# When the next block of dense weights is fetched ahead of the prompt's latent attention: a two-layer hybrid encoder on one core

## The chip, the core and the metric

The kernel is one program on one core of a Trainium2 chip. A core has TensorE (PE in the profile, with its weight loads as PEld), VectorE (DVE), ScalarE (ACT), GpSimd (POOL) and SyncE (SP). Each engine takes its own instructions in order and waits for the others by semaphores; transfers are issued by SP and by POOL. The metric is the device time of one execution in microseconds (us), as the median of several runs.

## The reference, cut to what matters

Two layers run over a prompt of 1024 tokens and over 8 samples of 16 tokens, 1152 tokens in all. All numbers are f32.

```python
xn   = rms_norm(x, g)                                  # 1024 features
proj = xn @ w_in[l]                                    # 7072 columns, split into
c_q, c_kv, k_r, z_mla, q_d, k_d, v_d, z_diff, x_lru, z_lru, gate_logits = pieces
# latent attention: 8 heads, chunk-causal, softmax over the visible keys
s     = q_lat . c_kv + q_rope . k_rope
o_mla = softmax(s * 96**-0.5) . c_kv -> w_uv, times silu(z_mla)
o_diff = ...                                           # differential attention, times silu(z_diff)
o_lru  = ...                                           # gated recurrence, times silu(z_lru)
g      = sigmoid(gate_logits)                          # 3 branches x 1024
x      = x + (sum_b g_b * (o_b @ w_o_b)) @ w_out
```

## The kernel before, in words

Every product that needs f32 accuracy is made of three matmuls: each operand is split into a high part and the rest (`hi`, `lo`), and hi·hi, lo·hi and hi·lo are added up in PSUM (lines 200 to 202 of the profile).

The projections that nobody needs at once (the four 128-column blocks of z for each branch and the eight 128-column blocks of gate logits for each branch) are *dense tasks*. They stand in one list, in a fixed order, and fill TensorE's time beside work that waits for other engines. A dense task has two parts. Its *load* (`wload`, line 230) fetches a weight block of 512 KB from `w_in` by one transfer on SP's queue into a staging tile `gs`, which has one buffer; ScalarE casts it to the high part `gh` (line 237, 128x1024); GpSimd subtracts in four pieces to get the low part `gl` (line 240). `gh` and `gl` have two buffers each. Its *run* goes over the 1152 tokens in three chunks of 384: 24 matmuls, then ScalarE's tanh from PSUM into a tile `th` (line 662 for a gate, line 637 for z), and a store of `th` by SP (line 663 for a gate, line 646 for z). `th` has four buffers, so the tanh of a chunk waits for the store of the fourth chunk before it to land.

`_advance` (line 86) does one step of the first task in the list. If the task has not begun it makes its load and begins it. Then it makes the load of the *second* task in the list, if that has not been made:

```python
        if len(self.tasks) > 1:
            self._load(self.tasks[1])
```

So one block is always fetched ahead. Who calls `_advance` is decided by credit: `weave` (line 149) interleaves generators and gives `fill` (line 115) some us of credit for each of their steps; `fill` advances dense tasks until the credit is used up.

An attention goes through `pipeline` (line 880). Work is cut into units (head h, query group g of 256 tokens); the scores of a unit run `lag` units ahead of its values. For the prompt's latent attention (`mla`, line 938) lag is 2 and `wide` is set. The order there is:

1. the loads of head 0 are issued on GpSimd's queue (`head`, line 953: parts of kT and qT, then V), and `fill(burst)` gives 13.5 us of credit at once: the *dense burst* (line 905);
2. the scores of units (0,0) and (0,1) are written, beside dense work;
3. `pause` (line 913) advances the running dense task to the end of its chunk, and from then on `wide` is 1: no dense work is given out, and the scores use five PSUM banks (three `sc`, two of the dense work's, named `scm`);
4. for the last two units `wide` is 0 again and dense work resumes (line 935).

In the burst of each layer the last z block of the latent attention's branch ends and gate block 0 of that branch, here G0, begins. G1, G2 and G3 are the gate blocks that follow. G0's own load is made well ahead, when the last z block begins.

The softmax of a score tile (`soft`, line 796) is a maximum on VectorE (line 811 with the mask, line 813 without) and an exponential on ScalarE (line 821, `P`). The tiles are then transposed on TensorE (`pt`, lines 838 to 845), split on ScalarE and VectorE (`ph`, `pl`), and multiplied with V (`po`, lines 860 to 864).

The code yields instructions with priorities, and a scheduler sets each engine's order from these by a plan of its own. A load that is written late can so stand early on its engine where it depends on nothing that comes late: G2's and G3's loads are written after the attention, but stand on SP before its first output.

Of the kernel before, what the change touches and what calls it, by code (L numbers as in the profile page):

```python
# [42 lines left out]
class Net:  # L43
# [23 lines left out]
    def __init__(self, ctx, tc, i, o, depth=DEPTH, only=None):  # L67
        self.ctx, self.tc, self.i, self.o = ctx, tc, i, o
        self.nc = tc.nc
        self.depth = depth  # L70
        self.only = only
        self.tasks, self.done, self.credit = [], set(), 0.0
        self.weight = [0.0] * 6
        self.turn = 0
        self.wide = 0
        self.under_way = False


    def add_task(self, key, load, run):
# [6 lines left out]
    def _advance(self):  # L86
        t = self.tasks[0]
        if t[4] is None:
            self._load(t)
            t[4] = t[2](*t[3])  # L90
        if len(self.tasks) > 1:
            self._load(self.tasks[1])
        try:
            return self.behind(self.LATER[0], t[4])
        except StopIteration:
            self.tasks.pop(0)
            self.done.add(t[0])
            return 0.0
# [781 lines left out]
    def pipeline(self, units, heads, prep, scores, values, us, burst=0.0, lag=1, steps=None, wide=False):  # L880

        keys = []
        for u in units:
            k, _ = heads(u)
            if k is not None and k not in keys:
                keys.append(k)
        gens = {}

        def start(j):
            if j < len(keys) and keys[j] not in gens:
                u = next(u for u in units if heads(u)[0] == keys[j])
                gens[keys[j]] = heads(u)[1]()

        def finish(k):
            if k in gens:
                self.weave([gens[k]], us)

        n = len(units)  # L900
        edge = self.EDGE
        start(0)
        if keys:
            next(gens[keys[0]])
            self.fill(burst)
            self.weave([gens[keys[0]]], edge)
        self.weave([prep(units[0])], edge)
        for k in range(lag):
            self.weave([scores(units[k])], edge)
            finish(heads(units[k + 1])[0])  # L910
            self.weave([prep(units[k + 1])], us)
        if wide:
            self.pause()
            self.wide = 1
        for k, u in enumerate(units):
            own, rates, later = [values(u)], [1.0], [self.LATER[2]]
            if k + lag < n:
                own = [scores(units[k + lag])] + own
                later = [self.LATER[1]] + later
                if steps:  # L920
                    rates = [1.0, steps(u)[1] / steps(units[k + lag])[0]]
                else:
                    rates = [1.0, 1.0]
            if k + lag + 1 < n:
                finish(heads(units[k + lag + 1])[0])
                own.append(prep(units[k + lag + 1]))
                rates.append(1.0)
                later.append(self.LATER[3])
            ahead = None
            if heads(u)[0] is not None:  # L930
                j = keys.index(heads(u)[0]) + 1
                start(j)
                ahead = gens[keys[j]] if j < len(keys) else None
            if k + lag >= n:
                self.wide = 0
            self.weave(own, 0.0 if self.wide else us if k + lag < n else edge, ahead, rates, later)
# [787 lines left out]
```

## Time and profile before

| what | value |
|---|---|
| median of 3 runs | 3026.06 us (3023.16 to 3031.2) |
| the profiled execution's own time | 3023.51 us |
| its span, first to last instruction | 3021.6 us |
| TensorE busy | 2857.7 us, 95% |
| VectorE busy | 1651.7 us, 55% |
| ScalarE busy | 1395.0 us, 46% |
| GpSimd busy | 772.8 us, 26% |
| transfers | 396.89 MB, mean 131 GB/s |

TensorE's share is near full in most of the 40 slices of the page, so a change elsewhere counts where TensorE stands still. The latent attention of the prompt begins at about 957 us in layer 0 and at about 2459 us in layer 1; "idle before" in a row is the time in which that engine stood still before the instruction, and the name behind the arrow is what it waited for. The granted clock of TensorE is shown as a share of full speed.

### The profile page before, as it was taken

To read this page: it belongs to the slowest core of one execution; us is meant where nothing else is said; L and a number is where in the kernel's file an instruction comes from. 1 tells how busy PE (TensorE), PEld (TensorE's weight loads), DVE (VectorE), ACT (ScalarE), POOL (GpSimd) and SP (SyncE) were. 2 spreads that over 40 slices of the span, in tenths; PEclk is the share of its full clock that TensorE was granted. 3 is DMA by queue.
4 is the path that set the end of the run, shared out by engine and by line. 5 is a ranking of instruction groups with operands and counts; after the bars stand their busy time and mean duration, and the time that the engine had idled before them with its cause. 6 is when DMAs were issued, how large, how long until landed. Compare 5 with 4: busy or idle time off the path is not lost. (4 is left out here: it accounts for less than half of the span.)

```text
span 3021.6 us, 50750 instructions
## 1 busy us (share of the span) xinstructions
PE 2857.7 (95%) x18466; PEld 2705.9 (90%) x18466; DVE 1651.7 (55%) x3947; ACT 1395.0 (46%) x3367; POOL 772.8 (26%) x1132
## 2 busy tenths in 40 slices
PE   7999999999998999999989999999999989999998
PEld 7899899999897888999989998999999978889998
DVE  6322878747255855555343328777561557545543
ACT  4433766646333765312234347666452447542121
POOL 2221335120102113352131313342101111133620
PEclk9999999999999999999999999999999999999999
DMA  5434545265248533764133345452642584427541
GB/s 168 129 98 106 125 111 140 69 180 164 75 124 246 123 81 84 220 184 162 63 116 125 92 116 126 113 142 64 190 141 79 161 215 119 95 76 231 171 156 73
DMA packets 387658, 396.89 MB, mean 131 GB/s; under 512 B 56192, under 2 KB 342496, under 8 KB 386344
## 3 DMA queue, kind: packets, MB, share of 16 engines
q1 hardware_dynamic: 368048, 331.70, 36.7%
q0 software_dynamic: 19360, 61.95, 9.2%
q8 instruction: 146, 2.39, 0.3%
q14 instruction: 104, 0.85, 0.1%
HBM read 265.89 MB, written 127.66 MB: 130 GB/s over the span
## 5 line engine op out<-in xcount | busy, mean ns | idle before, releaser
L200 PE MATMUL pg<-xh,gh 128*128 128x384 f32 x1152 | 401.2, 348 | 7.5 <-ACT th L662 7.5
L821 ACT ACTIVATE P<-sc,mx 128x384 f32<-128x384 f32 (+4 forms) x598 | 335.5, 566 | 130.7 <-DVE mx L811 100.2
L201 PE MATMUL pg<-xl,gh 128*128 128x384 f32 x1152 | 395.8, 344 | 0.0
L202 PE MATMUL pg<-xh,gl 128*128 128x384 f32 x1152 | 395.3, 343 | 0.0
L240 POOL TENSOR_TENSOR gl<-gs,gh 128x256 fp32r<-128x256 f32 x288 | 230.3, 829 | 585.8 <-ACT gh L237 527.3
L194 DVE TENSOR_TENSOR pl<-pt,ph 128x512 fp32r<-128x512 f32 (+1 forms) x320 | 199.6, 634 | 53.2 <-ACT ph L193 50.8
L200 PEld LDWEIGHTS pg<-xh,gh 128*128 128x128 f32 x1152 | 218.2, 189 | 11.4 <-ACT th L662 9.2
L201 PEld LDWEIGHTS pg<-xl,gh 128*128 128x128 f32 x1152 | 218.1, 189 | 2.7
L202 PEld LDWEIGHTS pg<-xh,gl 128*128 128x128 f32 x1152 | 218.1, 189 | 0.9
L193 ACT CAST ph<-pt 128x512 fp32r<-128x512 f32 (+1 forms) x320 | 169.5, 544 | 81.8 <-PE pt L845 80.1
L200 PE MATMUL z<-xh,gh 128*128 128x384 f32 x576 | 203.3, 353 | 0.0
L201 PE MATMUL z<-xl,gh 128*128 128x384 f32 x576 | 199.6, 346 | 0.0
L202 PE MATMUL z<-xh,gl 128*128 128x384 f32 x576 | 198.4, 344 | 0.0
L200 PE MATMUL sc<-wyh,xh 128*128 128x256 f32 x576 | 163.0, 283 | 5.8 <-DVE xt L1550 5.8
L200 PE MATMUL dp<-wh,xh 128*128 128x256 f32 x576 | 165.2, 287 | 3.4 <-ACT e L575 2.1
L201 PE MATMUL dp<-wl,xh 128*128 128x256 f32 x576 | 164.4, 285 | 0.8 <-POOL wl L555 0.8
L202 PE MATMUL dp<-wh,xl 128*128 128x256 f32 x576 | 164.3, 285 | 0.0
L202 PE MATMUL sc<-wyh,ml 128*128 128x256 f32 x576 | 162.9, 283 | 0.0
L201 PE MATMUL sc<-wyl,xh 128*128 128x256 f32 x576 | 162.9, 283 | 0.0
L1235 PE MATMUL sc<-kT,qT 98*128 98x384 f32 (+3 forms) x384 | 140.6, 375 | 5.2 <-ACT P L821 4.6
L240 POOL TENSOR_TENSOR wol<-wos,woh 128x128 fp32r<-128x128 f32 x192 | 101.0, 554 | 172.2 <-ACT woh L237 153.6
L813 DVE TENSOR_REDUCE mx<-sc 128x1 f32<-128x384 f32 (+2 forms) x200 | 116.0, 586 | 39.1 <-PE sc L202 21.0
(456 smaller groups left out, 8355.3 us busy)
## 6 DMA issues: line engine op xcount, KB each, us to landing
gs<-in_w_in_dram SPq DMA_DIRECT2D x72, 512.0 KB
ts<-th SPq DMA_DIRECT2D x144, 192.0 KB
th<-ts SPq DMA_DIRECT2D x144, 192.0 KB
K<-in_cache_diff_k_dram SPq DMA_DIRECT2D x64, 256.0 KB
Vt<-in_cache_diff_v_dram SPq DMA_DIRECT2D x32, 512.0 KB
u<-ob SPq DMA_DIRECT2D x48, 288.0 KB
ws<-in_w_in_dram SPq DMA_DIRECT2D x24, 512.0 KB
z<-th SPq DMA_DIRECT2D x48, 192.0 KB
```

The source lines that it names most:

```text
L193: nc.scalar.copy(hi, src)
L194: (lo_engine or nc.vector).tensor_tensor(lo, src, rr(hi), op=ALU.subtract)
L200: nc.tensor.matmul(out, ah, bh, start=start and k == 0, stop=False)
L201: nc.tensor.matmul(out, ah, bl, start=False, stop=False)
L202: nc.tensor.matmul(out, al, bh, start=False, stop=stop and k == n - 1)
L240: (lo_engine or nc.gpsimd).tensor_tensor(lo[:, k : k + half], st[:, k : k + half], rr(hi[:, k : k + half]), op=ALU.subtract)
L813: nc.vector.tensor_reduce(mx, sc[:, : n1 - n0], axis=AX.X, op=ALU.max, negate=True)
L821: nc.scalar.activation(P[:, n0:n1], scs[k][:, : n1 - n0], AF.Exp, bias=mx, scale=1.0 if adds[k] is None else -1.0, accum_out=l2[:, k : k + 1])
L1235: nc.tensor.matmul(ps, lhs, kT[:, m, n0:n1], start=True, stop=True)
```

## The change

A flag `hold` is set when the dense burst of a `wide` pipeline begins and is taken back after `pause`. While it is set, `_advance` does not make the load of the second task. The flag is false for the two other users of `pipeline`.

```diff
         self.under_way = False
+        self.hold = False
...
-        if len(self.tasks) > 1:
+        if len(self.tasks) > 1 and not self.hold:
             self._load(self.tasks[1])
...
             next(gens[keys[0]])
+            self.hold = wide
             self.fill(burst)
...
             self.pause()
+            self.hold = False
             self.wide = 1
```

One load per layer is made at another point of the program: G1's, which was made in the burst when G0 began, is now made when dense work resumes at the end of the attention. No instruction is added or taken away. The scheduler places the moved instructions by its plan, and this is where they stand in layer 0; layer 1 has the same rows with other numbers. Line numbers of the kernel with the change are one higher up to its line 905, and two or three higher behind it.

SP's queue, from the last stores of z (`z0_0_111`) to the weight blocks fetched ahead. Before, `gs_10568` is G1, `gs_12497` G2 and `gs_12822` G3; `ts0_0_121` are the stores of G0's three chunks:

```order
L646 DMA z0_0_111<-th_10403 128x384
L236 DMA gs_10568<-in_w_in_dram 128x8x128
L646 DMA z0_0_111<-th_10506 128x384
L646 DMA z0_0_111<-th_10535 128x384
L663 DMA ts0_0_121<-th_10609 128x384
L646 DMA z0_0_111<-th_10564 128x384
L663 DMA ts0_0_121<-th_10661 128x384
L663 DMA ts0_0_121<-th_10690 128x384
L236 DMA gs_12497<-in_w_in_dram 128x8x128
L236 DMA gs_12822<-in_w_in_dram 128x8x128
```

The same queue with the change, where `gs_12488` is G1:

```order
L647 DMA z0_0_111<-th_10403 128x384
L647 DMA z0_0_111<-th_10506 128x384
L647 DMA z0_0_111<-th_10535 128x384
L647 DMA z0_0_111<-th_10564 128x384
L237 DMA gs_12488<-in_w_in_dram 128x8x128
L664 DMA ts0_0_121<-th_10600 128x384
L664 DMA ts0_0_121<-th_10652 128x384
L664 DMA ts0_0_121<-th_10681 128x384
L237 DMA gs_12497<-in_w_in_dram 128x8x128
L237 DMA gs_12822<-in_w_in_dram 128x8x128
```

G1's fetch has moved behind three stores of z, and all four stores of z now stand ahead of G0's; the fetches of G2 and G3 keep their places.

ScalarE at the start of the attention before: G0's three tanh (`th<-pg`), the cast of G1 (`gh_10569`), the first exponentials (`P`), and among them the cast of G2 (`gh_12498`):

```order
L662 ACTIVATE th_10609<-pg_10577 128x384
L237 CAST gh_10569<-gs_10568 128x1024
L662 ACTIVATE th_10661<-pg_10612 128x384
L662 ACTIVATE th_10690<-pg_10664 128x384
L821 ACTIVATE P_10602,lsum_10474<-sc_10603,mx_10607 128x128
L821 ACTIVATE P_10620,lsum_10474<-sc_10621,mx_10625 128x256
L821 ACTIVATE P_10637,lsum_10474<-sc_10638,mx_10642 128x384
L237 CAST gh_12498<-gs_12497 128x1024
L821 ACTIVATE P_10654,lsum_10474<-sc_10655,mx_10659 128x512
L821 ACTIVATE P_10698,lsum_10474<-scm_10699,mx_10718 128x384
```

The same place with the change; G1's cast is `gh_12489`:

```order
L663 ACTIVATE th_10600<-pg_10568 128x384
L663 ACTIVATE th_10652<-pg_10603 128x384
L238 CAST gh_12489<-gs_12488 128x1024
L663 ACTIVATE th_10681<-pg_10655 128x384
L822 ACTIVATE P_10593,lsum_10474<-sc_10594,mx_10598 128x128
L822 ACTIVATE P_10611,lsum_10474<-sc_10612,mx_10616 128x256
L822 ACTIVATE P_10628,lsum_10474<-sc_10629,mx_10633 128x384
L822 ACTIVATE P_10645,lsum_10474<-sc_10646,mx_10650 128x512
L822 ACTIVATE P_10689,lsum_10474<-scm_10690,mx_10709 128x384
```

G1's cast stands one tanh later, and no cast stands among the first exponentials. G2's cast is now some 30 rows further on, within head 1:

```order
L822 ACTIVATE P_10953,lsum_10474<-sc_10954,mx_10964 128x384
L822 ACTIVATE P_10953,lsum_10474<-scm_10960,mx_10964 128x384
L877 COPY hv_10921<-po_10860 64x256
L238 CAST gh_12498<-gs_12497 128x1024
L822 ACTIVATE P_10975,lsum_10474<-sc_10976,mx_11004 128x512
```

Nothing else stands there on ScalarE but the attention's own exponentials and splits.

GpSimd before, from head 0's V on: four pieces of G1's low part (`gl_10570`), the loads of head 1 (`kT1`, `qT1`, `V`), those of head 2 (`kT0`, `qT0`), and G2's low part (`gl_12499`):

```order
L960 DMA V_10486<-vm0_95 128x1024
L240 TENSOR_TENSOR gl_10570<-gs_10568,gh_10569 128x256 x4
L957 DMA kT1_10477<-kn0_91 64x2048
L958 DMA qT1_10479<-qn0_87 64x2x1024
L959 DMA qT1_10479<-qr0_89 32x2x1024
L960 DMA V_10693<-vm0_95 128x1024
L957 DMA kT0_10476<-kn0_91 64x2048
L958 DMA qT0_10478<-qn0_87 64x2x1024
L959 DMA qT0_10478<-qr0_89 32x2x1024
L240 TENSOR_TENSOR gl_12499<-gs_12497,gh_12498 128x256 x4
L960 DMA V_10933<-vm0_95 128x1024
```

The same queue with the change, up to head 3's first load:

```order
L963 DMA V_10486<-vm0_95 128x1024
L960 DMA kT1_10477<-kn0_91 64x2048
L961 DMA qT1_10479<-qn0_87 64x2x1024
L962 DMA qT1_10479<-qr0_89 32x2x1024
L963 DMA V_10684<-vm0_95 128x1024
L960 DMA kT0_10476<-kn0_91 64x2048
L961 DMA qT0_10478<-qn0_87 64x2x1024
L962 DMA qT0_10478<-qr0_89 32x2x1024
L241 TENSOR_TENSOR gl_12490<-gs_12488,gh_12489 128x256 x4
L963 DMA V_10924<-vm0_95 128x1024
L241 TENSOR_TENSOR gl_12499<-gs_12497,gh_12498 128x256 x3
L960 DMA kT1_10477<-kn0_91 64x2048
```

Head 1's loads now follow head 0's V at once, G1's low part stands behind head 2's loads of k and q, and three pieces of G2's low part stand ahead of head 3's loads.

## Rows read from the trace of the kernel before

**Rows 1.** Who waited for whom, the whole run: total us, times, longest us.

```profile
ACT gh L237 <- DMA gs<-in_w_in_dram: 52.9, 14, 9.7
```

**Rows 2.** Timeline of ScalarE, 957 to 973 us: start us, us, engine, line, operation [idle before].

```profile
957.29 0.49 ACT L662 ACTIVATE th<-pg 128x384 f32<-128x384 f32 x1 [3.53 <-PE pg L202]
...
969.07 1.04 ACT L237 CAST gh<-gs 128x1024 fp32r<-128x1024 f32 x1 [9.24 <-DMA gs<-in_w_in_dram]
970.02 0.68 ACT L821 ACTIVATE P<-sc,mx 128x512 f32<-128x512 f32 x1
...
972.25 0.59 ACT L821 ACTIVATE P<-scm,mx 128x384 f32<-128x384 f32 x1
```

**Rows 3.** Timeline of TensorE, 961 to 971 us.

```profile
970.85 0.80 PE L200 MATMUL sc<-kT,qT 128*128 128x512 f32 x1 [9.20 <-ACT P L821]
```

**Rows 4.** Timeline of VectorE, 957 to 973 us.

```profile
959.63 0.70 DVE L811 CUSTOM_DVE_ANT_0 sc<-sc,mask 128x512 f32<-128x512 f32 x1 [0.51 <-PE sc L202]
...
962.63 0.14 DVE L811 DVE_READ_ACCUMULATOR2_ANT mx<- 128x1 f32 x1
972.53 0.69 DVE L813 TENSOR_REDUCE mx<-sc 128x1 f32<-128x512 f32 x1 [9.76 <-PE sc L202]
```

**Rows 5.** Busy time by stretch, PE, PEld, DVE, ACT, POOL; then granted clock, transfer share, GB/s.

```profile
961.65:970.85 9.20, 0.00 (x1) 0.01 (x1) 0.97 (x3) 1.78 (x4) 0.00 (x0) 0.70 0.70 177
970.85:975.70 4.85, 4.85 (x13) 4.00 (x14) 2.27 (x5) 2.80 (x10) 0.00 (x0) 0.50 0.00 0
...
2473.00:2477.50 4.50, 4.50 (x12) 3.72 (x13) 2.06 (x4) 2.45 (x10) 0.00 (x0) 0.50 0.00 0
```

**Rows 6.** Timelines of ScalarE and TensorE in layer 1, 2458 to 2474 us.

```profile
2471.11 1.04 ACT L237 CAST gh<-gs 128x1024 fp32r<-128x1024 f32 x1 [9.67 <-DMA gs<-in_w_in_dram]
...
2472.89 0.79 PE L200 MATMUL sc<-kT,qT 128*128 128x512 f32 x1 [9.62 <-ACT P L821]
```

**Rows 7.** Timeline of SP's queue, 940 to 983 us.

```profile
942.00 0.68 SPq L236 DMA_DIRECT2D gs<-in_w_in_dram  x1
942.74 6.32 SPq L646 DMA_DIRECT2D z<-th  x2
...
958.23 22.99 SPq L236 DMA_DIRECT2D gs<-in_w_in_dram  x2
...
980.84 0.38 SPq L236 DMA_DIRECT2D gs<-in_w_in_dram  x1
```

**Rows 8.** Timeline of GpSimd, 935 to 985 us.

```profile
949.98 0.55 POOL L960 DMA_DIRECT2D V<-vm  x1 [10.49 <-DMA vm<-f]
...
956.20 0.56 POOL L957 DMA_DIRECT2D kT<-kn  x1
...
957.87 0.56 POOL L960 DMA_DIRECT2D V<-vm  x1
976.33 0.53 POOL L957 DMA_DIRECT2D kT<-kn  x1 [17.90 <-PE sc L202]
...
977.99 2.82 POOL L240 TENSOR_TENSOR gl<-gs,gh 128x256 fp32r<-128x256 f32 x4
```

**Rows 9.** Timeline of ScalarE ahead of the attention and within head 1.

```profile
950.69 0.49 ACT L662 ACTIVATE th<-pg 128x384 f32<-128x384 f32 x1 [10.72 <-DMA z<-th]
952.33 1.05 ACT L237 CAST gh<-gs 128x1024 fp32r<-128x1024 f32 x1 [1.15 <-DMA gs<-in_w_in_dram]
...
991.20 0.37 ACT L876 COPY hv<-po 64x256 f32<-64x256 f32 x1
```

**Rows 10.** Transfers issued from 956 to 960 us: times, KB each, us to landing.

```profile
kT<-kn POOLq DMA_DIRECT2D x1, 512.0 KB, 4.8
...
V<-vm POOLq DMA_DIRECT2D x1, 512.0 KB, 9.6
```

**Rows 11.** Busy time by stretch, as in rows 5: G1's landing, and one head.

```profile
951.00:954.00 3.00, 2.77 (x10) 2.77 (x11) 0.00 (x0) 1.62 (x3) 0.54 (x1) 0.63 1.08 374
...
975.70:992.90 17.20, 15.83 (x114) 14.27 (x113) 13.46 (x34) 13.32 (x39) 5.05 (x8) 1.00 0.58 110
```

## The prediction

> **What bounds the kernel now.** I looked at the waits of the whole run first, for lines that the change touches. ScalarE's casts of dense weights waited for their own fetch 14 times, 52.9 us in all, and the longest of these waits is 9.7 us [rows 1]. Then I looked for where the long ones lie, in the timelines around the two starts of the prompt's latent attention. In layer 0 ScalarE does three exponentials, then stands 9.24 us in front of the cast of a weight block until 969.07, and only then comes to the 512-wide exponential at 970.02 [rows 2]. That exponential did not need the weights: its maximum was done on VectorE at 959.63 + 0.70 = 960.33 [rows 4]. ScalarE works in order, so the cast held up five exponentials, the PSUM banks that they read stayed full, and TensorE stood 9.20 us, until the first of them let go of a bank [rows 3]. VectorE stood 9.76 us [rows 4]. Behind the gap TensorE runs at half clock: 4.85 us busy at a granted 0.50, that is 1.2 GHz [rows 5]. Layer 1 has the same picture: ScalarE 9.67 us, TensorE 9.62 us, then 4.50 us at 0.50 [rows 5, 6]. TensorE bounds the run over nearly all of its length, so time that it stands still for two casts is time of the run.
>
> Which block is it? By the order it is G2, issued on SP at 958.23, right behind the four loads of head 1, which GpSimd issued from 956.20 to 957.87 [rows 7, 8]. It could go out only then because the staging tile was held until G1's low part was done on GpSimd. From issue to cast are 969.07 - 958.23 = 10.84 us.
>
> **The change part by part.** No instruction is added or removed. Three things move in each layer.
>
> First, G2's cast leaves the first exponentials. That is the gain. TensorE's gap goes: 9.20 us in layer 0, 9.62 us in layer 1. With the gap the half clock behind it goes: half of 4.85 and of 4.50 us, 2.43 and 2.25 us [rows 5]. The upper end is thus 11.63 + 11.87 = 23.5 us. What is late next is VectorE's chain of maxima: before, all five were waiting in store when ScalarE came, and now each exponential waits for its own. The last of the five began at 972.25; its maximum ended at 962.63 + 0.14 = 962.77 [rows 2, 4], and with the 0.59 us exponential of its pair in front it can begin near 963.4. That is 8.85 us earlier, the lower end for one layer if the clock gives nothing. Between 8.85 and about 11.7 I take 10.5, a little nearer the upper end, since TensorE's own rows are the ones that count in a stage where it is the busiest engine (15.83 of 17.20 us in the head that follows [rows 11]).
>
> Second, G2's cast stands within head 1 now. It takes 1.04 us of a ScalarE that is busy 13.32 of 17.20 us there [rows 11]; the cost is 0 to 1.05 us, and I take 0.3, because the idle quarter is in small pieces between exponentials. Does it wait for its fetch again? On GpSimd, G1's low part now follows head 2's loads. Those are released by head 0's last scores, at 976.33 before [rows 8], and 10.2 us earlier with the change: 966.1. Their issue takes 977.99 - 976.33 = 1.66 us and the four pieces 2.82 us, so SP can issue G2 at 970.6; before, the third block went out at 980.84 from exactly this chain [rows 7, 8]. The two slowest of these fetches took 952.33 - 942.00 = 10.33 and 10.84 us to their casts [rows 7, 9]. So G2 is there by 981.4 at the worst. ScalarE comes to the cast after the copy that stood at 991.20 [rows 9], now at 981.0 and 0.37 us long. The wait is 0 even then. Behind the cast wait three pieces of G2's low part, and behind them head 3's loads on GpSimd; these are wanted a whole head (17.20 us) after they are released, and the pieces take 2.1 us. That costs nothing.
>
> Third, G1's cast stands one tanh later, and its fetch behind three stores of z. What waits behind the cast is G0's third tanh, which TensorE releases at 957.29 [rows 2], and then every exponential. So the cast is free if G1 has landed by 956.2. Before, G1 was issued at 942.00; the next two stores needed until 949.06 to go out, and the cast ran at 952.33 [rows 7, 9]. The queue drains at the same time now, with 3 x 192 KB more in front of G1, at 374 GB/s [rows 11] 1.6 us: 953.9, 2.3 us ahead of need. The price is 0 to about 5 us (see the second way below); I take 0. Head 1's loads go out behind head 0's V, from 950.5 on (949.98 + 0.55) instead of 956.20, and lie beside G1's fetch. They are needed no later than before and gain nothing. G0's first tanh waits until 950.69 for a store of z that is ahead of all this [rows 9]; I leave that wait as it is.
>
> The sum: 2 x (10.5 - 0.3) = 20.4 us. The profiled execution took 3023.51 us, so it would be 3003.1; the median of the three runs, 3026.06, lies 2.55 us above that execution, so I predict 3005.7 us.
>
> Of queues the Trainium skill says, on its page "DMA: Bandwidth & Descriptors", section "Queues, rings and completion order", that each transfer engine goes round between the queue rows that have work, a packet at a time. By this G1 on SP's queue would share with head 1's loads on GpSimd's instead of coming ahead of them, which speaks against this change; the row on G2 (issued last, cast 1.6 us after the last of the four loads landed) agrees with that and with service in order of issue, so it does not decide. By the rule the sum would be the 3017 of the second way.
>
> **The rivals.** *The first way* is the sum: 3005.7 us, and by its ends 3000 to 3010, with the spread of runs to 3012.
>
> *The second way:* G1's fetch is shared out with head 1's loads and the stall moves one block forward. Before, the four loads took from 956.20 to 957.87 + 9.6 = 967.5, 11.3 us [rows 8, 10]; from 950.5 on they end at 961.8, and G1 with them. Then the cast (1.05), the third tanh (0.49) and three exponentials stand between that and the 512-wide one, which begins near 965.5 instead of 970.02. Each layer gains 4.5 us, the clock nothing: 3026.06 - 9 = 3017. For it speaks that G2 was slow in just such company. Against it: G1 is issued before those loads, a load on GpSimd's queue needs 4.8 us to land even as the first of its row [rows 10], and 1.6 us of backlog fits in before.
>
> *The third way:* the change doesn't do what it says. The scheduler still puts G1's fetch between burst and attention, only some stores later. If SP could not issue it before 955, a fetch of 10.84 us would land at 966 and the stop would be as long as now: 3026. Against it: SP had nothing to wait for there but room, and had that by 949.06.
>
> *The other side, slower:* G2's cast, now in mid-attention, waits there with all of ScalarE behind it. It decides from a landing after 981.4 + 10.2 = 991.6, which is 21 us after its issue; up to there the wait only eats the gain. At 25 us each layer loses 4 us net: 3034. For it: G2's chain now runs over TensorE's scores, GpSimd, SP and back, all within one head. Against it: 21 us is twice the slowest fetch here.
>
> **How the numbers follow.** First way 0.76, second 0.14, third 0.05, slower 0.05. A run of this kernel can be told from no change at about 0.3%, 9.1 us. The first way is faster; the second, at 9 us, half faster and half the same; the third the same. With a little of the first taken for a poor restart that makes 0.81 faster, 0.14 same, 0.05 slower. The range reaches from just under the upper end of the gain (3026.06 - 23.5 = 3002.6, less 3.6 for the spread of medians) to just over the second way: 2999 to 3018.
>
> **What would show it.** At each attention's start ScalarE has no cast among its first exponentials, TensorE no gap over 2 us between its first scores and head 0's values, and a granted clock of 1.00 in the 15 us that follow; G1's cast runs before G0's third tanh with a wait that ends by 956; G2's cast lies within head 1 with no wait for its fetch. Each attention is 10 us shorter, and nothing else changes by more than 1 us. The forecast is wrong if ScalarE waits over 3 us for G1 (second way) or for G2 in head 1 (slower), or if the gap closes and TensorE instead waits for VectorE's maxima through the first head, which would hold the gain under 8 us in each layer.

## The result: faster by 0.6%, with one layer of the profile as forecast and one not

The median of 12 runs is 3007.6 us against 3025.2 us for the kernel before, a ratio of 0.9942 with a 95% interval of 0.9926 to 0.9959. That is 17.5 us (12.4 to 22.4), where 20.4 were forecast: 3005.7, range 2999 to 3018. The profiled execution took 3005.46 us, its span 3003.7 us (before: 3023.51 and 3021.6). The two layers did not do the same, and the profile after is read layer by layer.

| from G0's first matmul to the attention's last scores | layer 0 | layer 1 |
|---|---|---|
| before | 159.13 us | 159.36 us |
| after | 155.49 us | 148.51 us |
| gain | 3.6 us | 10.9 us |

This length is from the start of the first matmul into `pg` to that of the last one out of kT and qT. It is used for every kernel below, since it holds all that the change moves; each gain is counted from the one profile of the kernel before. The two gains make 14.5 us; the other 3.4 of the 17.9 us between the spans lie in stages that the change doesn't touch.

**Layer 1** took the first way. This is ScalarE's timeline there (start us, us, engine, line, operation [idle before]); it answers to [rows 6].

```profile
2447.49 1.04 ACT L238 CAST gh<-gs 128x1024 fp32r<-128x1024 f32 x1 [2.24 <-DMA gs<-in_w_in_dram]
2450.84 0.49 ACT L663 ACTIVATE th<-pg 128x384 f32<-128x384 f32 x1 [2.31 <-PE pg L203]
...
2453.97 0.69 ACT L822 ACTIVATE P<-sc,mx 128x512 f32<-128x512 f32 x1 [0.58 <-DVE mx L812]
2454.55 0.19 ACT L822 ACTIVATION_READ_ACCUMULATOR P<-sc,mx 128x1 f32 x1
2455.10 0.58 ACT L822 ACTIVATE P<-scm,mx 128x384 f32<-128x384 f32 x1 [0.35 <-DVE mx L812]
```

G1's cast waits 2.24 us, but in time in which ScalarE has nothing else: behind it TensorE still works on G0's third chunk, and the third tanh waits 2.31 us for that. No cast stands among the exponentials; where one waits, it is for its own maximum, 0.2 to 0.6 us. TensorE's longest gap from there to 2462 us is 0.94 us.

**Layer 0** took the second way. ScalarE's timeline, in answer to [rows 2, 9]:

```profile
949.54 0.49 ACT L663 ACTIVATE th<-pg 128x384 f32<-128x384 f32 x1 [10.61 <-DMA z<-th]
953.32 0.49 ACT L663 ACTIVATE th<-pg 128x384 f32<-128x384 f32 x1 [3.29 <-DMA z<-th]
960.13 1.04 ACT L238 CAST gh<-gs 128x1024 fp32r<-128x1024 f32 x1 [6.32 <-DMA gs<-in_w_in_dram]
961.08 0.48 ACT L663 ACTIVATE th<-pg 128x384 f32<-128x384 f32 x1
...
964.55 0.69 ACT L822 ACTIVATE P<-sc,mx 128x512 f32<-128x512 f32 x1 [1.62 <-DVE mx L812]
```

Here G1's cast comes at 960.13, and the third tanh and every exponential stand behind it. TensorE's timeline, in answer to [rows 3]:

```profile
961.96 0.79 PE L201 MATMUL sc<-kT,qT 128*128 128x512 f32 x1 [4.67 <-ACT P L822]
```

The gap of 9.20 us is 4.67 us now, and half clock follows it as before. Busy time by stretch (PE, PEld, DVE, ACT, POOL; granted clock, transfer share, GB/s), in answer to [rows 5]; the first two stretches are layer 0, the last is layer 1:

```profile
955.90:960.90 5.00, 1.40 (x11) 1.07 (x9) 1.50 (x6) 0.77 (x1) 0.00 (x0) 1.00 1.01 296
960.90:967.70 6.80, 5.74 (x17) 5.34 (x18) 2.96 (x7) 3.94 (x14) 0.00 (x0) 0.50 0.09 33
...
2449.10:2458.50 9.40, 9.35 (x52) 7.86 (x51) 6.26 (x19) 6.02 (x19) 0.00 (x0) 1.00 0.98 216
```

In layer 1 TensorE is busy 9.35 of 9.40 us at a granted 1.00 in the stretch where layer 0 has first 1.40 of 5.00 us and then 6.8 us at 0.50, which is 1.2 GHz.

Why does the same program do both? SP's queue in the two layers, in answer to [rows 7], first layer 0 and then layer 1 (`vm` is the last store that belongs to V, then the four stores of z, then G1):

```profile
939.62 0.36 SPq L426 DMA_DIRECT2D vm<-f  x1
940.03 2.46 SPq L647 DMA_DIRECT2D z<-th  x4
942.59 0.44 SPq L237 DMA_DIRECT2D gs<-in_w_in_dram  x1
...
2434.87 3.44 SPq L647 DMA_DIRECT2D z<-th  x4
2438.41 0.44 SPq L237 DMA_DIRECT2D gs<-in_w_in_dram  x1
```

And GpSimd's timeline, in answer to [rows 8], head 0's V and head 1's loads in the two layers:

```profile
942.65 0.56 POOL L963 DMA_DIRECT2D V<-vm  x1 [4.33 <-DMA vm<-f]
943.20 0.53 POOL L960 DMA_DIRECT2D kT<-kn  x1
...
2443.68 0.56 POOL L963 DMA_DIRECT2D V<-vm  x1 [10.40 <-DMA z<-th]
2444.23 0.53 POOL L960 DMA_DIRECT2D kT<-kn  x1
```

In layer 1 head 1's first load goes out 2444.23 - 2438.41 = 5.8 us behind G1, and G1 is cast 9.1 us after its issue. In layer 0 it goes out 0.6 us behind, because the store that V waits for had landed early (942.65 where before V went out at 949.98 [rows 8]), and G1 is cast 17.5 us after its issue. The order is the same; what differs is a race between SP's stores and GpSimd's queue. G1 is not alone in it: the second tanh waits 3.29 us for a store of z.

G2 did what was forecast. Its cast stands in head 1, without a wait; ScalarE in layer 0:

```profile
986.49 0.37 ACT L877 COPY hv<-po 64x256 f32<-64x256 f32 x1
986.77 1.05 ACT L238 CAST gh<-gs 128x1024 fp32r<-128x1024 f32 x1
```

It was issued at 975.21, 11.6 us ahead of its cast. Over the whole run (total us, times, longest us; [rows 1] had 52.9, 14, 9.7):

```profile
ACT gh L238 <- DMA gs<-in_w_in_dram: 38.4, 12, 6.3
```

### The profile page after: what moved, and what is told of

Read it like the earlier page. It is cut to its first block, busy times and chain, and to the rows that moved or that the text cites. A ratio compares the mean times of both kernels' runs of the same rounds, so it can differ in the third digit from the quotient of the medians.

```text
span 3003.7 us, 50760 instructions
## 1 busy us (share of the span) xinstructions
PE 2854.4 (95%) x18466; PEld 2702.6 (90%) x18466; DVE 1651.8 (55%) x3947; ACT 1397.8 (47%) x3367; POOL 774.3 (26%) x1132
## 5 line engine op out<-in xcount | busy, mean ns | idle before, releaser
L201 PEld LDWEIGHTS pg<-xh,gh 128*128 128x128 f32 x1152 | 218.3, 190 | 11.3 <-ACT th L663 9.0
L663 ACT ACTIVATE th<-pg 128x384 f32<-128x384 f32 x144 | 70.4, 489 | 134.4 <-PE pg L203 97.9
```

Of the source, the lines that this page charges most:

```text
L201: nc.tensor.matmul(out, ah, bh, start=start and k == 0, stop=False)
L663: nc.scalar.activation(th, ps, AF.Tanh, scale=0.5)
```

## The experiments

Theory A: the gain is G2's cast leaving the first exponentials, 10.5 to 12 us in a layer; what layer 0 lacks is G1's fetch, slowed by head 1's loads where these go out close behind it. Rivals: layer 0's stall has another cause (B); weights fetched in mid-attention come too late (C); a good part of the gain comes from other things that moved, head 1's loads or the stores of z (D).

**The changed kernel again, four times**: two comparisons of six and eight executions, and two single executions, each with its profile.

> The changed kernel once more, to see whether its two layers always go as in its first profile (layer 1 without a stall, layer 0 with 6.3 us in front of the cast of G1). Theory A (a race decides: when the store that head 0's V waits for lands early, GpSimd sends V and head 1's four loads within 2 us of G1's fetch, which then takes 17 us instead of 10): a profile of another execution may show either outcome in either layer, but always the long fetch where V goes out within 2 us of G1, and the short one where V goes out 5 us or more behind it; the time is 3007 within 6 us. Rival B (layer 0's stall has another cause): the long fetch stands in layer 0 again, whenever V goes out. Ratio to before 0.994.

> The changed kernel a third time: two more layers to sort. Theory A: G1's fetch takes over 15 us exactly where head 0's V and with it head 1's four loads go out within 2 us of G1's issue, and 9 to 12 us where they go out 5 us or more later; a layer of the first kind is 3.6 us shorter than before from G0's first matmul to the attention's last scores, one of the second kind 10.5 to 11.2. The time is 3006 to 3011.

> One look at the changed kernel, for two more layers. Theory A: over 15 us for G1 only where head 1's loads go out within 2 us of it, and that layer gains 3.6 us; otherwise 9 to 12 us and a gain of 10.5 to 11.2 us.

> Another look at the changed kernel, with the same expectation as the look before it.

Measured: 0.9925 (0.9911 to 0.9939) and 0.9940 (0.9919 to 0.9962), medians 3010.4 and 3011.0 us against 3032.3 and 3027.7 us before; the two single executions took 3016.2 and 3019.5 us. With the first profile there are five of the same kernel and ten layers (second to fifth are the four runs above, in their order), sorted here by how far behind G1's issue head 1's first load goes out:

| profile, layer | head 1's first load behind G1's issue | G1's issue to its cast | length | gain |
|---|---|---|---|---|
| first, 0 | 0.6 us | 17.5 us | 155.49 us | 3.6 us |
| fourth, 1 | 3.8 us | 18.6 us | 155.67 us | 3.7 us |
| fifth, 0 | 4.4 us | 18.7 us | 155.62 us | 3.5 us |
| third, 0 | 5.8 us | 9.1 us | 148.37 us | 10.8 us |
| second, 1 | 5.8 us | 12.1 us | 148.14 us | 11.2 us |
| first, 1 | 5.8 us | 9.1 us | 148.51 us | 10.9 us |
| second, 0 | 5.8 us | 9.2 us | 148.65 us | 10.5 us |
| fifth, 1 | 5.9 us | 13.7 us | 148.99 us | 10.4 us |
| fourth, 0 | 6.0 us | 10.7 us | 148.16 us | 11.0 us |
| third, 1 | 6.4 us | 9.6 us | 148.74 us | 10.6 us |

By their lengths the ten fall into two kinds with nothing in between, and either layer can be of either kind. By G1's fetch alone they are less far apart: 13.7 us still costs nothing. Rival B, which ties the stall to layer 0, falls: in the fourth profile it is layer 1. Theory A stands, but not its bounds: "within 2 us" was too narrow, since 3.8 and 4.4 us behind is close enough, and its 9 to 12 us for the other kind were passed by 12.1 and 13.7. This is the fourth profile's layer 1, on GpSimd, ScalarE and TensorE (G1 was issued at 2435.32):

```profile
2438.60 0.56 POOL L963 DMA_DIRECT2D V<-vm  x1 [7.08 <-DMA vm<-f]
2439.15 0.53 POOL L960 DMA_DIRECT2D kT<-kn  x1
```

```profile
2453.92 1.04 ACT L238 CAST gh<-gs 128x1024 fp32r<-128x1024 f32 x1 [10.74 <-DMA gs<-in_w_in_dram]
```

```profile
2455.75 0.80 PE L201 MATMUL sc<-kT,qT 128*128 128x512 f32 x1 [5.94 <-ACT P L822]
```

ScalarE's idle time of 10.74 us holds the whole stall; TensorE loses 5.94 us of it and then some clock. Three layers in ten lose 7.1 us (10.75 less 3.6, the means of the two kinds); with three in ten as the share, an estimate from ten layers, the mean gain is 2 x (0.7 x 10.75 + 0.3 x 3.6) = 17.2 us. The three comparisons measured 17.5, 22.7 and 18.2 us. The rest of the run, the span less the two lengths, is 2699.7 to 2713.1 us in these five profiles of one kernel (before: 2703.2): the larger part of the spread between executions is not of the change's making.

Why do 4.4 us cost everything and 5.8 us nothing? The records of the packets tell. The profile counts SP's transfers as `q1 hardware_dynamic` and GpSimd's as `q0 software_dynamic` (packets, MB, share of the 16 transfer engines; a packet counts where it starts, so a share can pass 100%). Between head 0's loads of k and q and its V, GpSimd's queue has a pause, in which SP's stores of z and G1 behind them move alone. In the fifth profile's layer 0 the pause goes from 948.99 to 951.59:

```profile
q1 hardware_dynamic: 966, 0.96, 106.9%
q0 software_dynamic: 7, 0.00, 0.2%
```

From 952 to 961, with V and head 1's loads under way:

```profile
q0 software_dynamic: 523, 2.14, 91.6%
q1 hardware_dynamic: 525, 0.27, 28.6%
```

In its layer 1, which has no stall, the pause goes from 2451.24 to 2454.61:

```profile
q1 hardware_dynamic: 1470, 1.23, 108.9%
q0 software_dynamic: 8, 0.00, 0.2%
```

Side by side the two queues moved as many packets, but SP's have 0.5 KB and GpSimd's 4.1 KB in the mean: SP got 30 GB/s where alone it had about 370. At that rate the four stores and G1 (1.31 MB) need an estimated 3.5 us of pause. In the seven unhindered layers the pause lasted 3.2 to 3.6 us; 461 to 718 of G1's 1024 packets were through at its end, the rest 1.2 to 2.7 us later. In the three others it lasted 1.1, 2.2 and 2.6 us, with 0, 8 and 72 packets through, and G1's last packet came 0.8 to 1.6 us behind the last of V and head 1's loads. So head 0's V ends the pause, and head 1's loads right behind it make the sharing long. In the seven GpSimd's queue moved only 6 to 18 packets in the first half us behind the pause, in the three 32 to 37, and over half of what was left of G1 went in that half us; why the queue starts more slowly there is not shown.

**Head 1's loads held back** until G0's third tanh, by small copies into their tiles.

```diff
+                    self.th = th
...
+                if h == 1:
+                    for x in (kT[0:1, 0, 0:1], qT[0:1, 0, 0:1], qT[64:65, 0, 0:1], V[0:1, 0, 0:1]):
+                        nc.gpsimd.tensor_copy(x, self.th[0:1, 0:1])
                 nc.gpsimd.dma_start(kT[:64], self.kn[l][h * 64 : h * 64 + 64])
```

> The changed kernel with head 1's four loads held on GpSimd until G0's third tanh is done (957 us in layer 0), by four one-element copies into their tiles. Nothing of head 1 can then lie beside G1's fetch. Theory A: G1 lands within 10.5 us of its issue in both layers, the wait in front of its cast is under 1.5 us in both, and the 5 to 6 us that layer 0 lost come back: 3007.6 - 5.5 = 3002 us, 5 us less than the unchanged copy of this call. Rival B (what layer 0 lost is not the contention with head 1's loads): G1 still needs 15 us or more in layer 0, and the time is that of the copy, 3007. If holding the loads makes head 1's first scores wait instead, TensorE shows a wait for kT or qT of some us and the gain is smaller by it.

Measured: 0.9943 (0.9925 to 0.9962), 3014.6 us, 4.2 us over the copy of the changed kernel where 5 less were expected. G1 is cast 9.1 and 10.3 us after its issue, with idle times of 2.23 and 2.02 us that end 3.4 us ahead of the third tanh: the expectation of 1.5 us was too strict, but they cost nothing. The time did not come down, and the lengths are 150.51 and 150.77 us, 2 us over the unhindered kind. Head 1's loads now go out late, at 959.13, and TensorE waits for one of them (waits within 955 to 1005 us: total us, times, longest):

```profile
PE scm L201 <- DMA qT<-qr: 0.8, 1, 0.8
```

From head 2's loads to head 3's the held kernel needs 20.4 and 20.8 us, the changed one 19.3 in every profile. 0.8 us of that is this wait. Behind it TensorE, busy for 2.23 of the 4.00 us before in layer 0, has 3.4 us at half clock in both layers, which none of the unhindered layers has within its attention; in layer 0 (busy times as in the stretches above):

```profile
969.01:972.42 3.41, 3.41 (x16) 3.41 (x16) 1.79 (x7) 1.25 (x5) 0.00 (x0) 0.50 1.14 189
```

TensorE's matmuls of these heads stand in another order here too; what that costs by itself is not shown. So A is right on G1, and the remedy costs 2 us itself.

**Neither G1 nor G2 at the start**: G1's fetch waits for a value that head 4 writes.

```diff
+        if late:
+            nc.vector.tensor_copy(st[0:1, 0, 0:1], self.mark[0:1])
         nc.sync.dma_start(st, src[:, col : col + n].rearrange("(k p) n -> p k n", p=128))
...
+                if u == (4, 0):
+                    nc.vector.tensor_copy(self.mark[0:1], ots[0][0:1, 0:1])
```

> The changed kernel with G1's fetch made to wait for a value that head 4 writes, so that neither G1 nor G2 is fetched or cast at the attention's start; both are fetched in its second half. Theory A: no cast and no half clock stretch over 4 us at either start; each layer gains what layer 1 gained by the change, about 12 us: 3025.2 - 24 = 3001 us, 6 us less than the changed kernel. Rival B: layer 0's loss is not G1's cast, 3007. Rival C (the weights wanted at the resumption now come late): ScalarE or TensorE waits for gs or gh near the end of the attention, and the time is 3010 or more.

Measured: 0.9906 (0.9891 to 0.9921), 3006.7 us, 28.5 us less than before and 3.6 less than the copy of the changed kernel in the same comparison. The lengths are 147.07 and 145.45 us, gains of 12.1 and 13.9 us. Rival C falls: no cast of a gate block waits for its fetch in the attention of either layer.

**G2 alone**: the kernel before, with the same two edits for G2's block and nothing else. Run twice.

> The kernel before with one thing taken away: G2's fetch waits for a value that head 4 writes; G1 is fetched in the burst as before, and its stores of z, head 1's loads and G1's low part stand as before. Theory A (the gain is G2's cast leaving the first exponentials, and nothing else): 9.2 and 9.6 us of TensorE's standstill and half of the 4.9 and 4.5 us at half clock go in both layers, 3025.2 - 23 = 3002 us. Rival D (a good part of the change's gain comes from head 1's earlier loads or from the stores of z): less than half of it, 3014 or more.

> The kernel in which G2's fetch alone is held back, once more beside the changed kernel, to see whether it beats it: G1 is cast before G0's second tanh there and has no part in the race with head 1's loads. Theory A: 11.5 us in each layer in every execution, ratio 0.9915 to the kernel before; the changed kernel, with a layer in four going the short way, 0.993, so this one is 3 to 5 us faster. Rival B: both the same within 1 us.

Measured: 0.9909 (0.9893 to 0.9925) and 0.9913 (0.9895 to 0.9932), 3006.7 and 3003.2 us, where the changed kernel beside it had 3010.4 and 3011.0; the intervals overlap, so that it beats the changed kernel is not shown by the times alone. The four lengths are 147.77, 147.78, 147.82 and 148.23 us, gains of 11.1 to 11.6 us. All of the gain is there, though the stores of z stand as before and head 1's loads go out at 956.07 (before 956.20): rival D falls. No layer has a stall, since G1 is fetched behind the first store of z and head 1's loads wait for G1's low part. This kernel also shows what V alone does. In its layer 1 (SP, GpSimd, ScalarE):

```profile
2432.73 0.42 SPq L238 DMA_DIRECT2D gs<-in_w_in_dram  x1
```

```profile
2435.23 0.56 POOL L963 DMA_DIRECT2D V<-vm  x1 [4.82 <-DMA vm<-f]
...
2447.97 0.57 POOL L960 DMA_DIRECT2D kT<-kn  x1
```

```profile
2444.08 1.05 ACT L239 CAST gh<-gs 128x1024 fp32r<-128x1024 f32 x1 [2.37 <-DMA gs<-in_w_in_dram]
```

V goes out 2.5 us behind G1, in the range where the changed kernel stalls, but head 1's loads do not follow it, and G1 is cast after 11.4 us, in the second run after 11.7, without a stall; layer 0 has 8.7 and 8.4. The early V costs G1 some 3 us. What makes it 17.5 or more is the loads that follow it, with the stores of z that stand ahead of G1 in the changed kernel and here partly behind it.

**Head 1's loads of k and q ahead of V**, written with head 0's.

```diff
-                nc.gpsimd.dma_start(kT[:64], self.kn[l][h * 64 : h * 64 + 64])
...
+                for x in ((0, 1), (), (2,), (3,), (4,), (5,), (6,), (7,))[h]:
+                    nc.gpsimd.dma_start(kTs[x % 2][:64], self.kn[l][x * 64 : x * 64 + 64])
```

> The changed kernel with head 1's loads of k and q written with head 0's, so that they go out on GpSimd ahead of head 0's V, some 3 us ahead of G1's fetch instead of 5 us behind it, in both layers. Theory A (a fetch on SP's queue that meets head 1's loads is shared out with them): G1 now takes 15 us or more in both layers, ScalarE stands 4 us or more in front of its cast, and both layers gain 3 to 4 us instead of 10.5: 7 us in all against the kernel before, ratio 0.9976, 12 us more than the unchanged copy of this call. Rival B (layer 0's long fetch in the first profile had nothing to do with head 1's loads): G1 takes 9 to 12 us in both layers as in the other profiles and the time is that of the copy within 3 us.

Measured: 0.9953 (0.9937 to 0.9970), 3016.4 us, 5.3 us over the copy. They went out 7.1 and 3.9 us ahead of G1, not 3. G1's cast came 12.6 and 18.3 us after its issue, so one layer of the two as A said; but the time was lost one wait earlier. ScalarE and TensorE in layer 0:

```profile
955.54 0.97 ACT L663 ACTIVATE th<-pg 128x384 f32<-128x384 f32 x2 [16.02 <-DMA z<-th]
```

```profile
956.08 0.69 PE L201 MATMUL pg<-xh,gh 128*128 128x384 f32 x1 [8.88 <-ACT th L663]
```

The first tanh waits 16.02 us for a store of z where the changed kernel waits 10.61, and 18.06 us in layer 1; TensorE waits 8.88 us for it, where the changed kernel's layer 0 has 3.46. The loads on GpSimd's queue held up SP's stores as well as its fetch. In layer 1, from G1's issue to the end of the loads (2437.2 to 2451.8), the packets are again one for one:

```profile
q0 software_dynamic: 833, 3.29, 90.8%
q1 hardware_dynamic: 844, 0.64, 32.1%
```

The layers gain 6.3 and 3.4 us. The expected stall in front of G1's cast (2.15 and 2.20 us) did not come, because everything ahead of it was late already.

**Head 1's loads beside G1's fetch**, meant to force the collision: two small copies on VectorE, behind a chain of eight operations, release the loads of k and q. The two loads of V, head 0's too, come behind these and wait for G0's first tanh.

```diff
+                if h == 1:
+                    for _ in range(8):
+                        nc.vector.tensor_tensor(kT[0:64, 0, 0:384], self.zth[0:64], self.zth[0:64], op=ALU.subtract)
+                    for x in (qT[0:1, 0, 0:1], qT[64:65, 0, 0:1]):
+                        nc.vector.tensor_copy(x, rr(kT[0:1, 0, 0:1]))
                 nc.gpsimd.dma_start(kT[:64], self.kn[l][h * 64 : h * 64 + 64])
...
+                if h == 1:
+                    for x in (ops[0][2], V)[:2]:
+                        nc.scalar.copy(x[0:1, 0, 0:1], self.th0[0:1, 0:1])
+                    nc.gpsimd.dma_start(ops[0][2], self.vm[l][0].rearrange("p t x v -> p t (x v)"))
```

> The changed kernel with head 1's loads of k and q released some 4 us after the last z block's third chunk, by a chain of small copies on VectorE, and ahead of head 0's V on GpSimd, whose two V loads wait for G0's first tanh: the three loads so go out within 1 to 2 us of G1's fetch in both layers, behind the stores of z, which they no longer delay much. Theory A: G1 takes 15 us or more in both layers, ScalarE stands 4 us or more in front of its cast, TensorE starts its scores on half clock 5 us late, and each layer gains 3 to 4 us where the unhindered one gains 10.5; ratio 0.9976. Rival B (company does nothing to G1): 9 to 12 us in both layers, no stall, ratio 0.993.

It did not make the collision. VectorE's fills of kT and qT stand ahead of the chain until 948.9, and the loads went out at 954.20 (GpSimd):

```profile
954.20 0.53 POOL L968 DMA_DIRECT2D kT<-kn  x1 [15.85 <-DVE qT L967]
```

That is 10.5 and 10.7 us behind G1, which is a hold, of head 0's V too, and not a collision; for head 1's loads it is 4 to 5 us shorter than the first one. Read as such it is the better remedy by its lengths: G1 is cast after 9.4 and 9.0 us, the lengths are 148.06 and 148.51 us, and the ratio is 0.9922 (0.9906 to 0.9939), 3007.6 us. So a kernel that forces the collision at G1's issue was not had. That the loads slow G1 rests on the ten layers and their packets, the two holds, the early V without followers and the early loads.

Lengths against times, over all: the gains of the two profiled layers add up to 17.2 us for the first hold (measured 17.3), 21.9 for the second (23.7), 22.9 for G2 alone (27.6, interval 22.7 to 32.4), 22.4 the second time (26.3), 26.0 for neither (28.5) and 9.6 for the early loads (14.2, interval 9.1 to 19.1). Each sum lies within the interval of its time, so the two stretches can hold all of it. But the times fell by more in every one of these, by 0.1 to 4.7 us, while the rest of the run is no shorter in these profiles (2703.2 to 2714.0 us) than before (2703.2); where that comes from is open.

## Why the prediction was right, step by step

*G2's cast leaves the first exponentials.* Right in place and size. One reading was wrong, without effect on the sum: G2 was not held until 958.23 by the staging tile, since G1's low part was done at 956.25. SP's order held it, with G0's third store ahead of it, which waits for the tanh of 957.29 [rows 2]. The stall before was the cast's alone: with only that taken away the gain is 11.1 to 11.6 us in a layer, near the upper ends of 11.63 and 11.87. At head 2's loads the unhindered layers stand 11.3 to 12.1 us earlier (37.3 and 37.5 us after G0's first matmul before, 25.4 to 26.2 after), so the chain of maxima, which was to cost up to 2.8 us, costs none there. 1.0 us is given back on the way to head 4's loads: 36.0 instead of 35.0 us. The net 10.75 sits next to the 10.5 that was taken.

*G2's cast in head 1, 0.3 us.* No wait for the fetch, and no price that can be seen: with G2's cast taken out of head 1 the same stretch needs 36.3 us. So what is given back is not the cast's; TensorE's matmuls stand in another order in these heads, and whether that is it is not shown.

*G1's cast one tanh later, price 0.* Here the prediction failed in part. It had SP's queue drain "at the same time now", at 374 GB/s, and so G1 land by 953.9, and it put head 1's loads "from 950.5 on", taking V's release at 949.98 from one profile as a fixed time. The rate is right while GpSimd's queue pauses (370 GB/s) and wrong once V and head 1's loads go (30 GB/s), and when that is was left to chance. V's release is a race: V waits for a store on SP's queue, and in the ten layers it went out 3.0 to 9.5 us after SP had issued the last of those stores. Before, GpSimd had G1's low part between V and head 1's loads, so an early V released nothing behind it. The change took that away: moving G1's low part behind head 2's loads is what let head 1's loads follow V at once. In seven layers of ten the price is 0; in three it is 7.1 us, more than the about 5 us that it was to cost at most. The term should have been 0.3 x 7.1 = 2.1 us a layer, 4.3 in all, against the 0.55 us a layer by which the other two together were too small.

*The rivals.* The second way happened, with its mechanism and its price: G1 came in with the last of head 1's loads, and the three layers stand 4.4 to 4.6 us earlier at head 2's loads, as worked out; 1.0 us is given back behind that as in the others, which leaves 3.6. Its condition was left open: head 1's loads beside G1's fetch. What decides is whether V ends the pause of GpSimd's queue before the stores and half of G1 are through. And it was weighed as one outcome for both layers, where each layer goes its own way in each execution. The prediction's argument against it, 1.6 us of backlog ahead of G1, holds only where nothing from GpSimd comes into it. By the rule of the Trainium skill that was cited there, each transfer engine going round between queue rows a packet at a time, this is what an early V leads to; the trace agrees, with 523 packets of GpSimd's beside 525 of SP's in the fifth profile and 833 beside 844 with the loads put ahead. The third and the slower case did not occur: G2's fetch was there 11.6 us ahead of its cast.

*The sum.* 20.4 us against 17.5 (12.4 to 22.4) measured. The forecast would have been 17.2 with the race priced in, 3008.9 us. That the number came out so near owes something to luck: how often V would be early was not foreseen, and with both layers of the short kind the gain would be 7.2 us, 3018.9, just outside the range. The ends of the first way, 3000 to 3010, were taken from two bases, 3023.51 and 3026.06 us; from the median alone they are 3002.6 and 3010.5, which changes nothing here.

## What to carry to other kernels

An operation that is moved off a queue also releases what stood behind it there: look for the next instruction on each queue that the moved one used to hold back, and ask what it will run into. A release time read from one profile is one draw where it hangs on a store landing among other transfers; price both outcomes. And where one of two prefetches is the one in the way, hold back that one: G2 alone held has no stall in any of its four layers and gives 0.9909 and 0.9913, the change that moves both 0.9925 to 0.9942. Where two queues move packet for packet, look at the size of the packets: the one with the small ones gets the small share.

## What the runs showed of the chip

A 512 KB fetch on SP's queue took 8.4 to 13.7 us to its cast when head 1's loads (1.75 MB, three of them on 64 or 32 partitions) went out 5.8 us or more behind it, 11.4 and 11.7 us with one 128-partition load 2.5 and 3.0 us behind, and 17.5 to 18.7 us with the first of the four 0.6 to 4.4 us behind; G2's block in mid-attention, with three such loads 3.4 to 4.5 us *ahead* of it and none behind, landed after 5.4 to 6.8 us by its semaphore. Loads on GpSimd's queue also hold up stores on SP's: the first tanh's wait for a store of z was 10.0 to 10.8 us in all ten layers of the changed kernel, and 16.0 and 18.1 us with 1.25 MB of loads put ahead. The Trainium skill says on its page "DMA: Bandwidth & Descriptors", section "Queues, rings and completion order", that a transfer's semaphore is written only after every earlier write of the same transfer engine, across its queues; by this a small store could be told of late whenever loads lie ahead of it, but no run here shows it. These waits do not need it, since the store's own packets were late: they began 7.0 to 7.5 us after its issue in the changed kernel, and 12.6 and 13.0 us with the loads ahead, and the tanh began 0.8 to 1.6 us after the last of them had started. While both queues had work they moved one packet of SP's for about one of GpSimd's, of 0.5 and 4.1 KB.
